# Regrouping the small products of a recurrence, a gated mixer and state updates between large products on one Trainium2 core

## The chip, the cores and the metric

The kernel runs on one core of a Trainium2 chip. The metric is the device time of one execution in microseconds, lower is better. Five engines work side by side, each with its own queue of instructions: TensorE (PE; its weight loads are listed apart as PEld), VectorE (DVE), ScalarE (ACT), GpSimd (POOL) and SyncE (SP), which only issues DMAs here. They wait for one another through semaphores.

## What is computed

One layer of a hybrid diffusion backbone, for 512 latent tokens and 128 context tokens (640 tokens, feature width 1024). Four token mixers run in parallel on projections of the same normalized input, and a convolutional feed-forward network follows. Cut to what the change touches:

```
proj = h @ w_in                                   # 13 sections: a_x a_b a_c b_q b_ff b_fb b_i b_g c_q c_k c_v d_u d_v
y_b  = hgrn2_bidir(b_q, b_ff, b_fb, b_i, b_g)     # gated linear recurrence, forward and backward
y_c  = attention(c_q, c_k, c_v)                   # neighbourhood attention
y_d  = d_u * (ws @ rmsnorm(d_v) + b)              # chunked gated MLP, per group of 64 columns
merged = g_a*(y_a@w_br_a) + g_b*(y_b@w_br_b) + g_c*(y_c@w_br_c) + g_d*(y_d@w_br_d)
```

The recurrence keeps for each of 4 heads a state of 64 x 64 and returns the final states of the context tokens too. In chunks of 128 tokens it is

```
scores(t, s) = sum_d q[t,d] * k[s,d] * prod of the gates f between s and t     (s <= t; mirrored backward)
state'       = (product of the gates) * state + k_decayed^T v
out          = scores @ v + (q * decay) @ state
```

## The kernel before

**Large products.** A section of w_in (256 columns) is two units, each 16 groups of three products (high and low parts of a float32 number, `gemm_half`, L370, moving 320 columns; `tok_tile`, L937, moving 256). They follow one another on TensorE in the order ff fb q i g dv du ck cq cv ac ax ab. After each three products stands `tick(us)` (L101).

**Small products between them.** The mixers are Python generators. `tick` adds the estimated time of the three products to a clock, `now`, and lets every generator whose time has come do its next step; `yield x` says how long it rests (times a factor: 1.3 for the recurrence, 1.4 for the gated MLP). The time at which a step is due counts from the clock before the last step, and a step's own products move the clock too, by `pe(us)`:

```
    def step(j):
            j[0] = now[0] + (next(j[1]) or 0.0) * j[2]
```

So a step's small products stand in the program between two groups of three large ones, at a place set by the clock, which is a plan and no measurement. Outside the boot part and the part that begins in `g_all` (L1427), where the order is pinned, the framework then settles the order of instructions on each engine before the run, by its own estimate of when inputs and buffers are ready; an instruction that comes earlier in the program goes first when both are ready. At run time each engine works in that order and waits where something isn't there.

**The recurrence** (`hgrn`, L460) builds the scores in seven levels, l = 0 to 6. From level 1 on, for each head parity `par` (rows 0 to 63 or 64 to 127) 40 products of 64 rows by 32 columns are made (L539), each of which the trace records twice, being float32. At level 6 the products are 64 rows by 64 columns and come in four groups of 10, two halves `s0` with two parities each. Each parity's group goes into a PSUM bank of its own (`pm()`), of which there are four. VectorE then merges it into the scores through a mask (L544), and makes the next level's keys and queries from the present ones (L555 to L562), which the next level's products read. Between the parities the generator rests 0.4 (3 at level 4), after a level 5 (`HD[1]`).

Then the states: for four pairs of chunks (forward, backward) `kt_load` transposes the keys on TensorE (2 transposes, L579) and ScalarE copies them into one of two slots; `upd` multiplies them with the values (2 products, L588) and VectorE adds into the running state (L599). Then the outputs, one 128-token tile after another in the order 4, 1, 2, 0, 3 (L629 to L646), with their root mean squares on VectorE and GpSimd; then five pairs of transposes (L659 to L668).

**The gated MLP** (`gmlp`, L681): five token tiles with four products each of 128 rows by 64 columns (L700), whose result VectorE takes (L705). It begins behind section du and runs at the same time as the recurrence.

**First gated pair** (`g_pair0`, L1264), pinned. `gprod` (L1208) makes twelve products (four quarters k of three) for one of seven combinations, `bprod` (L1218) three. Around the touched place: the third product into bank b3, then combination 6 into bank p1_, which ScalarE copies to y, then combination 5 into c2_, then combination 7 added into p1_. That last one can't begin before p1_ has been copied.

```
        gprod(b3, 0, 3, True)
        ...
        bprod(p1_, 0, 6, False)
        oact(y[:, 0:HC], p1_, AF.Copy)
        ...
        bprod(c2_, 0, 5, True)
        bprod(p1_, 0, 7, False)
```

Of the kernel before, what the change touches and what calls it, by code (L numbers as in the profile page):

```python
# [69 lines left out]
def tile_step(ctx: ExitStack, tc: tile.TileContext, a: dict, outs: list, dbg=None):  # L70
# [244 lines left out]
    def rstd(out, ss, n, inv):  # L315
        vec.tensor_scalar(out, ss, inv, EPS, ALU.mult, ALU.add)
        pool.tensor_tensor(out, out, neghalf[:, 0:n], ALU.pow)  # L317
# [142 lines left out]
    def hgrn():  # L460
# [51 lines left out]
        for l in range(7):  # L512
            B = 1 << l
            e_, x_ = blk(kk[:, 0], B), blk(kk[:, 1], B)
            r_, p_ = blk(qq[:, 0], B), blk(qq[:, 1], B)
            f_, g_ = blk(ff[:, 0], B), blk(ff[:, 1], B)
            nb = 1280 // (2 * B)
            if l == 0:
                m = yield from along(near)
                vec.copy_predicated(nat, lmask[:, 0, :].unsqueeze(1).to_broadcast([P, 20, 32]), bc(m))  # L520

            W = 64 if l == 6 else 32
            ns = 320 // W
            for s0, par in ([(s_, r) for s_ in range(0, 10, ns) for r in range(2)] if l else ()):
                b = slice(64 * par, 64 * par + 64)
                m = pm()
                for i in range(s0, s0 + ns):
                    for g in range(P // W):
                        d, t0 = (0, W * g) if l < 5 else (1 - g % 2, W * (g ^ 1))
                        t0 += (i % 5) * P  # L530
                        k0 = i * P + W * g
                        rhs = qq[b, d, i // 5, t0:t0 + W]
                        if l < 5:
                            lhs = kl[b, k0:k0 + W]
                            rhs = bass.AP(rhs.tensor, rhs.offset,
                                          [list(rhs.ap[0]), [2 * B, 16 // B], [1280 + B, 2], [1, B]])
                        else:
                            lhs = f2(kk[:, g % 2])[b, k0:k0 + W]
                        mm(m[W * g:W * g + W, (i - s0) * W:(i - s0 + 1) * W], lhs, rhs,  # L539
                           start=True, stop=True, tile_position=(64 * par, W * g))  # L540
                    pe(0.18)
                mv = m[:, 0:ns * W].rearrange("p (i t) -> p i t", t=W)
                if l < 5:
                    vec.copy_predicated(near_at[:, par], lmask[:, l, :].unsqueeze(1).to_broadcast([P, 10, 32]), mv)  # L544
                else:
                    for g in range(P // W):
                        c = slice(W * g, W * g + W)
                        act(at[c, par, s0:s0 + ns, W * (g ^ 1):W * (g ^ 1) + W], mv[c], AF.Copy)
                if par == 0:
                    yield 3 if l == 4 else 0.4  # L550
            if l == 4:
                for g in range(4):
                    c = slice(32 * g, 32 * g + 32)
                    act(at[c, :, :, c].rearrange("p r i t -> p (r i) t"), nat[c], AF.Copy)
            ups = ((e_[:, :, 0, :], f_[:, :, 1, 0:1]), (x_[:, :, 1, :], g_[:, :, 0, 0:1]),  # L555
                   (p_[:, :, 1, :], f_[:, :, 0, 0:1]), (r_[:, :, 0, :], g_[:, :, 1, 0:1]))
            for i, (dst, mul) in enumerate(ups):
                vec.tensor_tensor(dst, dst, mul.to_broadcast([P, nb, B]), ALU.mult)
                if i == 1 and l < 4:
                    kl = keys(l + 1)  # L560
            fa = ff.rearrange("p d n t -> p (d n t)").rearrange("p (n j i) -> p n j i", j=2, i=B)
            vec.tensor_tensor(fa[:, :, 0, 0], fa[:, :, 0, 0], fa[:, :, 1, 0], ALU.mult)  # L562
            yield HD[1]
# [36 lines left out]
                                                 tot[b, d, pr, t:t + 1], u, ALU.mult, ALU.add)  # L600

        assert "i_done" in R
        for f, bwd in ((0, 3), (1, 2), (2, 1), (4, 4)):
            kt_load(0, f, 0)
            kt_load(1, bwd, 1)
            yield 1.5
            upd(0, f, 0)
            upd(1, bwd, 1)
            yield 1
        for par in range(2):  # L610
            for d in range(2):
                nc.sync.dma_start(o_st[0, 0, d, par::2].rearrange("h k v -> k h v"),
# [12 lines left out]
                              ALU.mult)  # L625

        last = None
        for t in (4, 1, 2, 0, 3):
            m = pm()  # L629
            for pr in range(2):  # L630
                if t < 4:
                    o = m[:, pr * P:(pr + 1) * P]
                    mm(o, qq[:, 1, pr, t * P:(t + 1) * P], sreg[:, 0, t, pr, :], start=True, stop=False,
                       skip_group_check=True)
                    mm(o, qq[:, 0, pr, t * P:(t + 1) * P], sreg[:, 1, t, pr, :], start=False, stop=False,
                       skip_group_check=True)
                    pe(0.43)
                for par in range(2):
                    h = pr * 2 + par
                    mm(m[:, h * 64:(h + 1) * 64], at[:, par, pr * 5 + t, :],  # L640
                       vt[:, t * 256 + h * 64:t * 256 + (h + 1) * 64],
                       start=(t == 4), stop=(t == 4 or par == 1), skip_group_check=True)
                    pe(0.21)
            act(og[:, t * 256:(t + 1) * 256], m[:, 0:256], AF.Copy)
            act(o2[:, t * 256:(t + 1) * 256], m[:, 0:256], AF.Square)
            yield 0.5  # L646

            s4 = ss[:, 4 * t:4 * t + 4]
            vec.tensor_reduce(s4, o3(o2, t), AX.X, ALU.add)
            rstd(s4, s4, 4, 1.0 / 64)  # L650
            if last is not None:
                normed(last)
            last = t
        R["hgrn_out"] = True
        yield 2.5
        normed(last)
# [2 lines left out]
        for t in range(5):  # L659
            m = pm()  # L660
            for pr in range(2):
                ten.transpose(m[:, pr * P:(pr + 1) * P],
                                    og[:, t * 256 + pr * P:t * 256 + (pr + 1) * P], ident)
                pe(0.11)
                s = sg[:, pr * T + t * P:pr * T + (t + 1) * P]
                vec.scalar_tensor_tensor(s, m[:, pr * P:(pr + 1) * P],
                                         p1[:, C_HN + pr:C_HN + pr + 1], s, ALU.mult, ALU.mult)
            yield 0.4  # L668
        nc.sync.dma_start(ybd, split_y("D", sg).bitcast(F32))
        R["hgrn_done"] = True  # L670
        R["yd"] = split_y("E", R["yt"])
# [9 lines left out]
    def gmlp():  # L681
        du = R["DX0"][:, 0:1280]
        x1 = R["DX1"]
        vg, yt = x1[:, 0:1280], x1[:, 1280:2560]
        gg = region("G", [P, 1280])
        wst, brow = gg[:, 0:512], gg[:, 512:768]
        nc.sync.dma_start(wst, a["gmlp_ws"])
        for g in range(4):
            nc.sync.dma_start(brow[64 * (g % 2):64 * (g % 2) + 64, (g // 2) * P:(g // 2 + 1) * P],
                              a["gmlp_b"][0, g, :].partition_broadcast(64))  # L690
        ss = dss
        rstd(ss[:, 0:5], ss[:, 0:5], 5, 1.0 / 256)
        for t in range(5):
            v = vg[:, t * 256:(t + 1) * 256]
            vec.tensor_scalar(v, v, ss[:, t:t + 1], None, ALU.mult)
        yield 6
        for t in range(5):
            m = pm()
            for g in range(4):
                mm(m[64 * (g % 2):64 * (g % 2) + 64, (g // 2) * P:(g // 2 + 1) * P],  # L700
                   vg[:, t * 256 + 64 * g:t * 256 + 64 * g + 64], wst[:, g * P:(g + 1) * P],
                   start=True, stop=True)
                pe(0.21)
            for pr in range(2):
                vec.scalar_tensor_tensor(yt[:, pr * T + t * P:pr * T + (t + 1) * P],  # L705
                                         m[:, pr * P:(pr + 1) * P],
                                         p1[:, C_GN + pr:C_GN + pr + 1],
                                         brow[:, pr * P:(pr + 1) * P], ALU.mult, ALU.add)
            yield 0.4
        vec.tensor_tensor(yt, yt, du, ALU.mult)  # L710
        R["yt"] = yt
        pool.dma_start(ydd, yt)
# [492 lines left out]

    omm = Ordered(nc.tensor).matmul

    def gprod(o, p_, i, first):  # L1208
        u, n = GPROD[i]
        w = gw[p_, u]  # L1210
        xh_, xl_ = gx["x"][i]
        for k in range(4):
            for j, (h, x) in enumerate(((0, xh_), (0, xl_), (1, xh_))):
                omm(o, w[:, h, n, k, :], x[:, k, :], start=(first and k == 0 and j == 0),
                   stop=(k == 3 and j == 2), skip_group_check=True)
# [48 lines left out]
    def g_pair0(r):  # L1264
# [38 lines left out]
        g_sig(0, 0, ga[:, HC:T], ga[:, HC:T])  # L1303
        ovec.tensor_tensor(gb[:, HC:T], b2, gb[:, HC:T], ALU.subtract)
        r[2] = gp_load(2)
        gprod(b3, 0, 3, True)
        g_al(1, r[1])
        y = gw[0, "y"] = gp.tile([P, T], F32, tag="gt", name=nm("y"))
        c2_ = gw[0, "b2"] = pm()[:, 0:HC]
        bprod(p1_, 0, 6, False)  # L1310
        oact(y[:, 0:HC], p1_, AF.Copy)
        ovec.tensor_tensor(gb[:, 0:HC], b3, gb[:, 0:HC], ALU.add)
        bprod(c2_, 0, 5, True)
        bprod(p1_, 0, 7, False)
# [1345 lines left out]
```

## Time and profile before

| | before |
|---|---|
| median of 3 runs | 996.89 us (996.79 to 997.28) |
| the profiled execution | 997.16 us, its span 995.3 us |
| TensorE clock granted | 0.998 of full speed |
| recurrence's levels (L539) on TensorE | first product at 111.0 us, last at 158.2 us |
| gated MLP's products (L700) | 150.6 to 158.8 us |
| state updates (L579, L588) | 164.4 to 179.3 us |
| outputs (L633 to L640) | 180.3 to 190.0 us |
| transposes (L662) | 201.1 to 205.2 us |
| pair 0 (`g_pair0`) begins | 275.0 us |

How to read it: times in the trace count from the start of the span. In the timeline, a row has the start, the time covered, the engine, the line, the operation, what is written and read, the rows and columns of the array (64*32), the moving operand and the number of instructions. Lines of helpers that pin the order all appear as L150. Large products follow one another more closely than they last, since they are pipelined, so the distances of their starts are what counts.

### The profile page before, as it was taken

Reading aid. Unit: us, or ns where it says so; the run is one execution under the profiler, and the core shown is the slowest. Engines: PE = TensorE matmul, PEld = TensorE weight load, DVE = VectorE, ACT = ScalarE, POOL = GpSimd, SP = SyncE. Lnnn points to the kernel's source line nnn. Section 1 sums busy time; section 2 is a strip of 40 time slices with the busy share of each in tenths; the row PEclk is TensorE's granted clock in tenths of the full one; section 3 lists DMA queues with packets and bytes.
Section 4 is the critical chain, followed back from the end, with each engine's and each line's share of the span. In section 5 each row is a group of like instructions: output and inputs, shape, how many; then the busy total and the mean of one; then the engine's idle time right before and its main releaser. Section 6 shows DMA issues by size and latency. Waiting matters only on the chain.

```text
span 995.3 us, 19011 instructions
## 1 busy us (share of the span) xinstructions
PE 983.9 (99%) x7437; PEld 932.0 (94%) x7437; DVE 862.3 (87%) x1411; ACT 592.2 (59%) x1034; POOL 198.9 (20%) x272
## 2 busy tenths in 40 slices
PE   8999999999999999999999999999999999999997
PEld 6899999999999999999998899999999999888886
DVE  5779899879988789898877788999999998999796
ACT  6652343355575565555655476877777777756672
POOL 1000023414123122333300021322222222100004
PEclk9999999999999999999999999999999999999999
DMA  9886449898179789999958684766666666976842
GB/s 353 333 282 252 130 131 282 236 277 269 52 255 278 202 214 312 254 267 279 271 195 341 248 321 136 221 172 167 177 171 162 177 171 194 361 265 201 297 133 106
DMA packets 76857, 227.54 MB, mean 229 GB/s; under 512 B 10560, under 2 KB 25440, under 8 KB 74080
## 3 DMA queue, kind: packets, MB, share of 16 engines
q1 hardware_dynamic: 44832, 149.91, 42.8%
q0 software_dynamic: 31936, 76.43, 32.3%
q8 instruction: 58, 0.95, 0.4%
q14 instruction: 31, 0.25, 0.1%
HBM read 185.26 MB, written 61.36 MB: 248 GB/s over the span
## 4 chain that ended last, share of the span: by engine, by line
PE 93%; DVE 3%; DMA 2%; POOL 1%; issue 1%; ACT 0%; SPq 0%; POOLq 0%
PE m L150 22%; PE g L1728 21%; PE g L374 12%; PE m L2191 9%; PE m L1728 5%; PE g L150 5%; PE m L1480 4%; PE g L2191 4%; PE g L955 2%; PE g L1480 1%; PE m L539 1%; PE m L1723 1%; DMA A<-in_w_ada_dram 1%; PE m L882 1%; POOL hss L317 1%
## 5 line engine op out<-in xcount | busy, mean ns | idle before, releaser
L374 PE MATMUL g<-XH,w 128*128 128x320 f32 x576 | 140.5, 318 | 0.0
L374 PEld LDWEIGHTS g<-XH,w 128*128 128x128 f32 x576 | 98.8, 188 | 2.2 <-issue 1.0
L150 PE MATMUL m<-XH,w 128*128 128x320 f32 x416 | 98.7, 311 | 0.0
L374 PE MATMUL g<-XL,w 128*128 128x320 f32 x288 | 89.1, 310 | 0.0
L150 PEld LDWEIGHTS m<-XH,w 128*128 128x128 f32 x416 | 70.8, 188 | 1.7 <-ACT XH L150 0.6
L150 PE MATMUL m<-XL,w 128*128 128x320 f32 x208 | 63.0, 310 | 0.0
L2191 PE MATMUL m<-w,XH 128*128 128x512 f32 x246 | 58.5, 390 | 0.0
L2191 PEld LDWEIGHTS m<-w,XH 128*128 128x128 f32 x246 | 46.1, 188 | 9.6
L374 PEld LDWEIGHTS g<-XL,w 128*128 128x128 f32 x288 | 54.3, 188 | 0.3 <-issue 0.2
L150 DVE TENSOR_TENSOR w<-raw,w 128x640 fp32r<-128x640 f32 (+3 forms) x47 | 48.4, 1047 | 1.6 <-ACT w L150 1.5
L150 POOL DMA_DIRECT2D wsum<-in_w_dn_dram x36 | 37.6, 1275 | 59.2 <-issue 38.0
L150 ACT ACTIVATE w<-raw 128x640 fp32r<-128x640 f32 (+3 forms) x53 | 48.3, 931 | 1.8 <-DMA raw<-in_w_in_dram 1.5
L150 DVE SCALAR_TENSOR_TENSOR X<-X,p2t,X 128x641 f32<-128x641 f32 x44 | 38.8, 883 | 0.9
L150 DVE SCALAR_TENSOR_TENSOR X<-MG,p2t,X 128x641 f32<-128x641 f32 x44 | 38.9, 883 | 0.8
L150 PEld LDWEIGHTS m<-XL,w 128*128 128x128 f32 x208 | 38.6, 188 | 0.6 <-issue 0.6
L1728 PE MATMUL g<-XL,w 128*128 128x320 f32 x240 | 38.7, 310 | 0.0
L1728 PE MATMUL g<-XL,C 128*128 128x320 f32 x240 | 38.3, 309 | 0.0
L150 ACT ACTIVATE gb<-m 128x320 f32<-128x320 f32 x32 | 14.0, 437 | 40.7 <-PE m L150 40.6
L1728 PEld LDWEIGHTS g<-XL,w 128*128 128x128 f32 x240 | 35.9, 188 | 0.9 <-ACT MG L2088 0.4
L1728 PEld LDWEIGHTS g<-XL,C 128*128 128x128 f32 x240 | 36.0, 188 | 0.0
L150 ACT ACTIVATE X<-X,p2t 128x641 f32<-128x641 f32 x22 | 20.4, 927 | 18.7 <-DVE X L150 18.7
L150 ACT ACTIVATE X<-g 128x320 f32<-128x320 f32 x30 | 13.1, 436 | 30.3 <-PE g L1728 30.3
(622 smaller groups left out, 2948.5 us busy)
## 6 DMA issues: line engine op xcount, KB each, us to landing
wsum<-in_w_dn_dram POOLq DMA_DIRECT2D x30, 512.0 KB, 14.2
raw<-in_w_gp_dram SPq DMA_DIRECT2D x23, 640.0 KB, 7.7
raw<-in_w_up_dram SPq DMA_DIRECT2D x28, 512.0 KB, 5.3
raw<-in_w_in_dram SPq DMA_DIRECT2D x19, 512.0 KB, 5.5
H<-in_w_adt_dram SPq DMA_DIRECT2D x19, 512.0 KB, 4.7
G<-in_w_up_dram SPq DMA_DIRECT2D x12, 512.0 KB, 5.2
raw<-wsum SPq DMA_DIRECT2D x12, 512.0 KB, 5.9
actx<-X POOLq DMA_DIRECT2D x22, 256.0 KB, 4.9
```

Source lines behind the costliest of these rows:

```text
L150: r = f(*args, **kw)
L317: pool.tensor_tensor(out, out, neghalf[:, 0:n], ALU.pow)
L374: mm(o, w[:, h, k0 + k, :], r(k)[:, s], start=(k == 0 and i == 0), stop=(k == kt - 1 and i == 2))
L539: mm(m[W * g:W * g + W, (i - s0) * W:(i - s0 + 1) * W], lhs, rhs, start=True, stop=True, tile_position=(64 * par, W * g))
L882: mm(mo[64 * hh_:64 * hh_ + 64, 0:P], v, ptt[(u + hh_) % 4][:, j * P:(j + 1) * P], start=(j == 0), stop=(j == 2))
L955: mm(o, x(kx)[:, ts], w[:, h, k, :], start=(kx == 0 and i == 0), stop=(kx == 7 and i == 2))
L1480: mm(m, mh[MHN[q]][:, hx, k % 2, t * P:(t + 1) * P], wo[q][:, hw, k % 2, :], start=(k == 0 and i == 0), stop=(k == 7 and i == 2))
L1723: mm(o, w[:, k, :], x[:, k, :], start=(first and not part and k == 0 and j == 0), stop=(part == 1 and k == 3), skip_group_check=True)
L1728: z = mm(o, w[:, k, :], x[:, k, :], start=(first and k == 0 and j == 0), stop=(k == 3 and j == 2), skip_group_check=True)
L2191: mm(ps, s[t // 4][:, hx, k, o:o + P], w[:, hw, k, c0:c1], start=first, stop=i == 2 and bi == len(batch) - 1 and k == len(ks) - 1, skip_gr ...
```

## The change

The same instructions are issued, in other groups. In the levels, the rest between the parities stays only at level 4 and once at level 6. In the state updates, the update of one pair of chunks and the transposes of the next go into one step. The outputs go in groups of one, two and two token tiles, the last transposes and the gated MLP's tiles in groups of two, two and one with twice the rest. In `g_pair0`, the last quarter of the third product is issued behind combination 6.

```diff
-                if par == 0:
-                    yield 3 if l == 4 else 0.4
+                if (l, par) == (4, 0):
+                    yield 3
+                elif (l, par, s0) == (6, 1, 0):
+                    yield 0.4
...
-        for f, bwd in ((0, 3), (1, 2), (2, 1), (4, 4)):
-            kt_load(0, f, 0)
-            kt_load(1, bwd, 1)
-            yield 1.5
-            upd(0, f, 0)
-            upd(1, bwd, 1)
-            yield 1
+        ends = ((0, 3), (1, 2), (2, 1), (4, 4))
+        for i in range(5):
+            for d in range(2):
+                if i:
+                    upd(d, ends[i - 1][d], d)
+            for d in range(2):
+                if i < 4:
+                    kt_load(d, ends[i][d], d)
+            yield 1 + 1.5 * (i < 4)
...
-        for t in (4, 1, 2, 0, 3):
+
+        def outs(t):
             m = pm()
...
             act(o2[:, t * 256:(t + 1) * 256], m[:, 0:256], AF.Square)
-            yield 0.5
-
-            s4 = ss[:, 4 * t:4 * t + 4]
-            vec.tensor_reduce(s4, o3(o2, t), AX.X, ALU.add)
-            rstd(s4, s4, 4, 1.0 / 64)
-            if last is not None:
-                normed(last)
-            last = t
+
+        for ts_ in ((4,), (1, 2), (0, 3)):
+            for t in ts_:
+                outs(t)
+            yield 0.5 * len(ts_)
+            for t in ts_:
+                s4 = ss[:, 4 * t:4 * t + 4]
+                vec.tensor_reduce(s4, o3(o2, t), AX.X, ALU.add)
+                rstd(s4, s4, 4, 1.0 / 64)
+                if last is not None:
+                    normed(last)
+                last = t
...
-            yield 0.4
+            if t % 2 or t == 4:
+                yield 0.8
...
-    def gprod(o, p_, i, first):
+    def gprod(o, p_, i, first, ks=range(4)):
...
-        for k in range(4):
+        for k in ks:
...
-        gprod(b3, 0, 3, True)
+        gprod(b3, 0, 3, True, range(3))
         g_al(1, r[1])
...
         bprod(p1_, 0, 6, False)
         oact(y[:, 0:HC], p1_, AF.Copy)
+        gprod(b3, 0, 3, True, range(3, 4))
         ovec.tensor_tensor(gb[:, 0:HC], b3, gb[:, 0:HC], ALU.add)
```

The edit of the rest (`if t % 2 or t == 4`) stands twice, in the recurrence's transposes and in `gmlp`.

More of the change, by code (lines that the diff above doesn't have):

```diff
@@ L708, in gmlp @@
                                          brow[:, pr * P:(pr + 1) * P], ALU.mult, ALU.add)
-            yield 0.4
+            if t % 2 or t == 4:
+                yield 0.8
         vec.tensor_tensor(yt, yt, du, ALU.mult)
```

## The prediction

> **What bounds the kernel now.** I read the page first (busy shares), then the stretch from 120 to 160 us by the table of windows, then the timeline of TensorE visit by visit, and last the chain that ended last and the list of waits.
>
> ```profile
> span 995.3 us, 19011 instructions
> ## 1 busy us (share of the span) xinstructions
> PE 983.9 (99%) x7437; PEld 932.0 (94%) x7437; DVE 862.3 (87%) x1411; ACT 592.2 (59%) x1034; POOL 198.9 (20%) x272
> ```
> ```profile
> 120.00:160.00 40.00, 40.00 (x876) 36.31 (x864) 40.00 (x78) 18.65 (x37) 12.20 (x17) 1.00 0.56 175
> ```
>
> TensorE has work for 983.9 of 995.3 us, so time can only be won by making its stream denser. The second row is the stretch in which most of the touched products lie: PE 40.00 of 40 us, its weight loads 36.31, and VectorE (the third engine) also 40.00. TensorE sets the pace there, but VectorE has no reserve at all. That is the main danger.
>
> The profiled execution took 997.16 us: the span of 995.3 and 1.86 around it. It lies 0.27 over the median of 996.89. I work out differences in the span and take them from the median.
>
> **What a visit costs.** I call a run of small products between two large ones a visit. Its price: from the start of the last large product before it to the start of the second one after it, less two spacings of large products. The second one is needed because the slow start after a visit shows only there. First the recurrence's products (L539), which use 64 rows by 32 columns of the array; spacing of the 256-column products around them is 0.12 (119.17 to 119.29).
>
> ```profile
> 110.79 0.28 PE L955 MATMUL m<-w,XH 128*128 128x256 f32 x1
> 111.00 0.89 PE L539 MATMUL m<-C,D 64*32 64x32 f32 x80
> 111.82 0.38 PE L955 MATMUL m<-w,XH 128*128 128x256 f32 x1
> 112.04 0.28 PE L955 MATMUL m<-w,XL 128*128 128x256 f32 x1
> ```
> ```profile
> 119.17 0.28 PE L955 MATMUL g<-w,XL 128*128 128x256 f32 x1
> 119.29 0.28 PE L955 MATMUL g<-w,XH 128*128 128x256 f32 x1
> 119.50 0.64 PE L539 MATMUL m<-C,E 64*32 64x32 f32 x50
> 120.06 0.39 PE L955 MATMUL g<-w,XH 128*128 128x256 f32 x1
> 120.29 0.28 PE L955 MATMUL g<-w,XL 128*128 128x256 f32 x1
> ```
>
> 80 records cost 112.04 - 110.79 - 0.24 = 1.01 us, 50 cost 120.29 - 119.29 - 0.24 = 0.76. So a record costs 0.25 / 30 = 0.0083, and a visit 1.01 - 80 x 0.0083 = **0.34 us before its first product**. One sees it in the rows: 0.21 instead of 0.12 before the visit, 0.22 instead of 0.12 after the first large product. Now products on the whole array (transposes L579, state updates L588), with a spacing of 0.15 (154.70 to 154.85 in the fence on level 6 below):
>
> ```profile
> 164.21 0.31 PE L374 MATMUL g<-XH,w 128*128 128x320 f32 x1
> 164.35 0.60 PE L579 MATMUL m<-cst,B 128*128 128x128 f32 x4
> 164.71 0.39 PE L374 MATMUL g<-XH,w 128*128 128x320 f32 x1
> 164.94 0.30 PE L374 MATMUL g<-XL,w 128*128 128x320 f32 x1
> ```
> ```profile
> 166.39 0.31 PE L374 MATMUL g<-XH,w 128*128 128x320 f32 x1
> 166.54 1.05 PE L588 MATMUL m<-E,D 128*128 128x128 f32 x8
> 167.35 0.39 PE L374 MATMUL g<-XH,w 128*128 128x320 f32 x1
> 167.58 0.31 PE L374 MATMUL g<-XL,w 128*128 128x320 f32 x1
> ```
>
> 4 records cost 0.43, 8 cost 0.89: 0.115 each and 0.43 - 4 x 0.115 = -0.03, that is **nothing for the visit itself**. So only groups of products that use part of the array can gain by being put together.
>
> **The change part by part.**
>
> *Levels of the recurrence (L524 to L550).* At levels 1, 2, 3 and 5 the groups of both parities (80 records each) go into one visit; level 4 keeps two. Four visits fewer: 4 x 0.34 = **-1.36 us**. No instruction is added or dropped, and both parities read the same inputs, so no new wait arises at the second one. What the trace doesn't show is the step from rows 0 to 63 to rows 64 to 127 inside a 64x32 visit: between 0 and 0.34 (a whole visit's price, then the gain is nothing). I take 0, from the nearest row, the visit of level 6 below with 64x64: it holds both row halves (40 records, 1.24 us) and is no dearer per record than one half (20, 0.78). [...]
>
> *Level 6 and the gated mixer's products (L700).* Before, these share visits:
>
> ```profile
> 152.84 0.31 PE L374 MATMUL g<-XH,w 128*128 128x320 f32 x1
> 153.08 0.85 PE L539 MATMUL m<-C,B 64*64 64x64 f32 x20
> 153.86 0.66 PE L700 MATMUL m<-G,X 128*64 128x128 f32 x8
> 154.45 0.42 PE L374 MATMUL g<-XH,w 128*128 128x320 f32 x1
> 154.70 0.31 PE L374 MATMUL g<-XL,w 128*128 128x320 f32 x1
> 154.85 0.31 PE L374 MATMUL g<-XH,w 128*128 128x320 f32 x1
> 155.16 1.31 PE L539 MATMUL m<-C,B 64*64 64x64 f32 x40
> 156.40 0.66 PE L700 MATMUL m<-G,X 128*64 128x128 f32 x8
> ```
>
> 20 records take 0.78 to the next kind, 40 take 1.24: 0.023 each, and 0.32 left over at the change of kind (at least part of it a slow start, so 0.1 to 0.32). Before: five visits (the mixer's five token tiles), three of them with such a change. After: three mixer visits and two of level 6. If they fall apart, five visits and no change of kind: -0.3 to -0.96. If two coincide, two visits and one change fewer: -0.8 to -1.0. I take **-0.7**.
>
> *State updates (L603 to L609), outputs (L628 to L646), transposes (L659 to L668).* 8 visits become 5, 5 become 3, 5 become 3, all on the whole array: by the fence above **0**. What is late next: a visit of updates now asks for four of the four small PSUM banks, and two of them come free only when VectorE has done L599. Bounds -0.2 (the one wait of TensorE for VectorE in the transposes, quoted below, goes) to +0.4 (twice that wait at new places); I take 0.
>
> *Third product's last quarter (L1306).* Three products of 0.15 us move behind L1310, before L1313.
>
> ```profile
> 288.28 0.60 PE L150 MATMUL g<-MG,w 128*128 128x320 f32 x3
> ```
> ```profile
> 288.99 0.56 ACT L150 ACTIVATE ga<-ga,cst 128x320 f32<-128x320 f32 x1 [1.05 <-DVE ga L150]
> ```
> ```profile
> 289.45 0.42 ACT L150 ACTIVATE y<-g 128x320 f32<-128x320 f32 x1
> 289.93 0.71 PE L150 MATMUL g<-MG,S 128*128 128x320 f32 x3 [0.60 <-ACT y L150]
> ```
>
> TensorE waits at 289.93 for ScalarE's copy of y, because the next product writes the bank that is copied. The product that fills it (288.28) is over at 288.88 and would now be over 0.44 earlier. But y stands behind the sigmoid of ga in ScalarE's fixed order, and that waits for VectorE. The same 18 products lie ahead of the waiting one in either order, so it arrives no later and waits as long. **0**, bounds -0.44 (were the copy waiting for TensorE after all) and 0.
>
> Sum of the gains: 1.36 + 0.7 = 2.06 us.
>
> **What VectorE takes back.** The step list counts a step's own products toward its pause. A level's pause is 5 x 1.3 = 6.5; its last step now holds two groups of 1.8 instead of one, so 2.9 are left instead of 4.7. At 0.41 per three large products that is 8 threes instead of 12. The 12 stand in the chain that ended last as 36 products:
>
> ```profile
> 129.28 5.48 PE g L374 x36
> ```
>
> With the three between the parities gone, each of four level distances (1 to 2, 2 to 3, 3 to 4, 5 to 6) shrinks by 5 threes, 5 x 0.44 = 2.2 us, together 8.8. VectorE, full from 120 to 160, prepares each level's keys and queries and can't follow. The levels' products will be due up to some 9 us before their operands. What then? Instructions here that aren't pinned are ordered ahead of the run by an estimate of when their inputs are ready, and the trace shows that this works. The attention's sixth step, paced like the others, stood behind 40 large products where the one before had 21, in a stretch where VectorE was late too:
>
> ```profile
> 249.13 3.28 PE g L374 x21
> ```
> ```profile
> 254.72 6.06 PE g L374 x40
> ```
> ```profile
> PE m L662 <- DVE MG L666: 0.2, 1, 0.2
> ```
>
> So I expect large products to be put ahead, and only the error of that estimate to remain as a wait. The nearest measured wait of that kind is the third row, 0.2 us. Four levels become tight, and two further meetings (banks of the updates): between 0 and 6 x 0.2 = 1.2; I take three of six, **+0.6**.
>
> Forecast: -2.06 + 0.6 = -1.5 us, 996.89 - 1.5 = **995.4**. All that comes later moves along: the attention is started behind the last cv product (L929), not at the recurrence's end.
>
> **Rivals.**
> 1. *The gain comes whole.* VectorE's estimate fits, the 0.2 at L662 goes, the two mixer visits coincide: -2.06 - 0.2 - 0.3 = -2.6, 994.3. For it: in the old order the waits list has no L539 at all. Against: VectorE had just enough time then.
> 2. *VectorE becomes the bound (slower).* If the order keeps the levels at their due place, TensorE, which works in order, stands before L539 until VectorE has finished L558 of the level before, and with it every large product behind. Price up to the 8.8 us by which the levels move up; with the gain -2.06 that is +6.7, 1003.6 at the end and 999.2 if half is overtaken. It decides from 4.1 us of waiting on (2.06 + 2.0). Against it: the 40 products above.
> 3. *The change doesn't do what it says.* The ordering splits the groups again, as it already did with a level's 80 records (50 above). Then visits stay as many and the time stays: 996.9. For it: two parities need two free banks at once. Against: four banks, and the mixer and the recurrence share them already.
>
> **How the numbers follow.** Forecast (994.9 to 996.6) 0.47; rival 1, below 994.9, 0.28; rival 3 and small losses up to 998.9, 0.10; rival 2 beyond that 0.15. A measurement of this kernel tells about 0.2%, 2.0 us, from no change: faster means below 994.9, slower above 998.9. So faster 0.28, same 0.57, slower 0.15. The range 993.8 to 999.2 leaves out the best twentieth and most of rival 2.
>
> **What would show it.** Right: L539 in visits of 160 records at levels 1, 2, 3 and 5, each about 0.0083 x 160 + 0.34 = 1.67 us; L700 in groups of 16; L588 and L579 side by side with 0.115 a record as before; the wait at g<-MG,S still 0.6. Wrong: a visit of 160 dearer than 1.9 us (the row change has a price); TensorE in the waits list with L539 and VectorE, more than 1 us (rival 2 sets in); the wait for y gone (then it hung on TensorE). More than 2 us of difference after 300 us, where nothing was changed but the quarter, would mean that the ordering changed elsewhere, which I count at nothing.

## The result and the profile after

The changed kernel takes 1009.1 us (median, 1007.7 to 1010.6) against 996.8 (996.6 to 997.3): 1.0123 times as long, with an interval of 1.0105 to 1.014. The forecast was 995.4. The profiled execution has a span of 1007.3 us, 12.0 more than before. All times here and below are medians of undisturbed executions; one of levels_123_paced, the only one of that kernel with a trace, took 1948 us and is left out.

From the page of the changed kernel: the span, the busy times, and the granted clock in 40 slices of 25 us. Then the stretch that the prediction began with, from the table of windows.

```profile
span 1007.3 us, 19021 instructions
...
PE 987.8 (98%) x7437; PEld 934.8 (93%) x7437; DVE 862.9 (86%) x1411; ACT 593.7 (59%) x1034; POOL 197.9 (20%) x272
...
PEclk9999989999999999999999999999999999999999
```
```profile
120.00:160.00 40.00, 37.17 (x742) 35.34 (x742) 35.66 (x65) 19.84 (x41) 12.31 (x18) 0.91 0.57 165
```

The same 7437 products are there, and VectorE (DVE) works as long as before (862.9 for 862.3). But between 120 and 160 us both engines now stand still at times (37.17 and 35.66 of 40), and TensorE's clock is 0.91 instead of 1.00: they wait for one another in turn. Of the 876 records in this stretch only 742 are done. The list of TensorE's waits (in total, times, longest) names the places; of before it held, of the regrouped products, only 0.2 us at the transposes and the 0.6 us for y.

```profile
PE m L539 <- issue: 2.1, 1, 2.1
PE m L590 <- DVE D L601: 2.1, 1, 2.1
PE g L150 <- DVE F L150: 1.6, 1, 1.6
PE m L671 <- DVE MG L675: 1.5, 1, 1.5
PE m L876 <- DVE X L873: 1.3, 2, 1.1
...
PE m L539 <- DVE C L560: 0.6, 2, 0.4
```

The third row is of the start and was there before. The last one is the wait that the prediction counted on, of the levels' products for VectorE: 0.6 us in all. (Line numbers have moved: updates L588 are L590, transposes L579 are L581, VectorE's L599 is L601, the mixer's L700 is L710, the last transposes L662 are L671.)

**The visits themselves cost what the prediction said.** The timeline of level 1: 160 records in one visit.

```profile
110.16 0.28 PE L966 MATMUL m<-w,XH 128*128 128x256 f32 x1
110.37 1.58 PE L539 MATMUL m<-C,D 64*32 64x32 f32 x160
111.88 0.39 PE L966 MATMUL m<-w,XH 128*128 128x256 f32 x1
112.11 0.28 PE L966 MATMUL m<-w,XL 128*128 128x256 f32 x1
```

112.11 - 110.16 - 0.24 = 1.71 us against 1.67 forecast and 2.02 for the two of before (levels 1, 3 and 5 came as 160 records, level 2 as 14 and 146). The loss lies elsewhere. Level 3, and the clock behind it:

```profile
121.13 0.28 PE L966 MATMUL m<-w,XH 128*128 128x256 f32 x1
121.76 1.63 PE L539 MATMUL m<-C,D 64*32 64x32 f32 x132 [0.35 <-DVE C L560]
125.53 0.64 PE L539 MATMUL m<-C,D 64*32 64x32 f32 x28 [2.14 <-issue]
```
```profile
124.00:126.00 2.00, 0.47 (x28) 0.47 (x28) 0.69 (x3) 0.00 (x0) 0.00 (x0) 0.70 0.75 229
126.00:128.00 2.00, 2.00 (x20) 1.94 (x11) 1.78 (x4) 0.21 (x1) 0.00 (x0) 0.50 0.13 41
128.00:130.00 2.00, 2.00 (x10) 2.00 (x9) 2.00 (x4) 2.00 (x5) 0.00 (x0) 0.50 0.00 0
130.00:132.00 2.00, 2.00 (x10) 1.92 (x9) 2.00 (x4) 0.14 (x2) 0.00 (x0) 0.60 0.00 0
```

TensorE waits 0.35 us for VectorE, does 132 of the 160 records, stops for 2.14 us while the profile shows nothing that it waits for ("issue"), and its clock is at half (third number from the right: 0.50) for 6.8 us, from 124.8 us on, still inside the stop: 0.3 / 0.5 of the first row, two full rows, 0.4 / 0.5 of the last. A second low stretch, of 3.4 us, begins at 172.6. In the kernel before the clock stayed at 1.00 from 16 to 990 us. The third place, the state updates, on TensorE and on VectorE:

```profile
168.74 0.31 PE L374 MATMUL g<-XL,w 128*128 128x320 f32 x1
171.12 0.71 PE L590 MATMUL m<-E,D 128*128 128x128 f32 x4 [2.07 <-DVE D L601]
```
```profile
164.96 1.13 DVE L715 SCALAR_TENSOR_TENSOR X<-m,cst,G 128x128 f32<-128x128 f32 x4
168.70 1.23 DVE L284 SCALAR_TENSOR_TENSOR junk<-H,S 128x1024 bf16<-128x1024 f32 x1 [2.61 <-DMA H<-in_w_adt_dram]
169.85 0.08 DVE L284 DVE_READ_ACCUMULATOR junk<-H,S 128x1 f32 x1
169.85 2.46 DVE L601 SCALAR_TENSOR_TENSOR D<-D,tot,m 64x64 f32<-64x64 f32 x8
```

TensorE waits for L601, which frees a bank. L601 stands behind L284, a step of the modulation columns (`ada_cols`, L239), whose input H is still being loaded: VectorE does nothing for 2.61 us.

The mixer's groups, and the wait for y in pair 0, as the prediction named them:

```profile
161.31 0.31 PE L374 MATMUL g<-XH,w 128*128 128x320 f32 x1
161.54 1.09 PE L710 MATMUL m<-G,X 128*64 128x128 f32 x16
162.57 0.41 PE L374 MATMUL g<-XH,w 128*128 128x320 f32 x1
162.82 0.30 PE L374 MATMUL g<-XL,w 128*128 128x320 f32 x1
...
301.95 0.70 PE L150 MATMUL g<-MG,S 128*128 128x320 f32 x3 [0.69 <-ACT y L150]
```

A mixer visit of 16 costs 1.22 us where two of 8 cost 1.58, and the wait for y is 0.69 for 0.60.

**Where the time went.** The table adds up, from the timeline, the price of every visit as the prediction defined it, by kind, from the same large product at 99.1 us to the same one at 258.6 us (times of before); "large" is what the spacing of large products exceeds its normal value by, elsewhere. All in us; the kernels of the experiments are in it too.

| | median | levels 1-5 | level 6, mixer, updates | outputs | transposes | attention | large |
|---|---|---|---|---|---|---|---|
| before | 996.8 | 10.66 | 12.21 | 8.05 | 1.64 | 18.29 | 0.68 |
| after | 1009.1 | 12.66 | 16.58 | 8.04 | 3.03 | 19.80 | 3.13 |
| levels_only | 1006.9 | 12.51 | 14.71 | 8.05 | 3.21 | 19.35 | 2.24 |
| levels_paced | 997.9 | 10.08 | 12.05 | 8.05 | 1.63 | 19.69 | 0.69 |
| updates_only | 997.6 | 10.66 | 13.43 | 8.05 | 1.36 | 18.28 | 0.65 |
| mixer_only | 1001.6 | 10.66 | 15.20 | 8.45 | 1.85 | 18.27 | 0.65 |
| outputs_transposes_quarter | 998.1 | 10.66 | 12.24 | 8.05 | 2.80 | 18.62 | 0.69 |
| all_but_levels | 999.6 | 10.64 | 14.73 | 8.10 | 1.25 | 18.62 | 0.74 |
| shift_plus | 1008.6 | 9.40 | 16.57 | 8.05 | 3.22 | 19.86 | 2.19 |
| levels_123_near | 1003.9 | 9.69 | 13.50 | 8.05 | 1.89 | 23.96 | 1.24 |
| near_column_later | 997.3 | 9.69 | 13.32 | 8.05 | 1.75 | 18.29 | 0.66 |
| whole_change_paced | 996.8 | 10.06 | 12.14 | 8.05 | 1.26 | 19.61 | 0.74 |
| whole_paced_column | 996.4 | 10.07 | 12.14 | 8.05 | 1.27 | 18.33 | 0.72 |

A row of the table is one execution, the traced one, and the median is of all. After against before: 2.0 + 4.4 + 0 + 1.4 + 1.5 + 2.45 = 11.7 us. A large product lies 0.63 us earlier than before at 99 us, 11.10 later at 258.6 and 12.04 later at 297; from there to the end nothing is added.

### The profile page after: what moved, and what is told of

It reads as the page before. It is cut to its first block, busy times and chain, and to the rows that moved or that the text cites. A ratio compares the mean times of both kernels' runs of the same rounds, so it can differ in the third digit from the quotient of the medians.

```text
span 1007.3 us, 19021 instructions
## 1 busy us (share of the span) xinstructions
PE 987.8 (98%) x7437; PEld 934.8 (93%) x7437; DVE 862.9 (86%) x1411; ACT 593.7 (59%) x1034; POOL 197.9 (20%) x272
## 4 chain that ended last, share of the span: by engine, by line
PE 86%; DVE 6%; DMA 3%; issue 2%; POOL 1%; ACT 1%; SPq 0%; POOLq 0%; DVEq 0%
PE m L150 21%; PE g L1740 21%; PE m L2203 9%; PE g L374 9%; PE m L1740 5%; PE g L150 5%; PE m L1492 4%; PE g L2203 4%; PE g L966 2%; PE g L1492 1%; PE m L1735 1%; DMA A<-in_w_ada_dram 1%; DMA H<-in_w_adt_dram 1%; DVE junk L284 1%; DMA X<-in_w_adt_dram 1%
## 5 line engine op out<-in xcount | busy, mean ns | idle before, releaser
L2102 DVE TENSOR_TENSOR w<-raw,w 128x1024 fp32r<-128x1024 f32 (+1 forms) x26 | 29.1, 1118 | 2.6 <-ACT w L2098 2.6
```

Source lines behind the costliest of these rows:

```text
L2102: vec.tensor_tensor(w[:, 1, 0:n], raw, w[:, 0, 0:n].bitcast(F32), ALU.subtract)
```

## The experiments

**The parts alone.** First the levels as in the change, the levels with a longer rest behind them, the state updates as in the change, and the change without the levels.

The kernel before, with (levels_only)

```diff
-                if par == 0:
-                    yield 3 if l == 4 else 0.4
+                if (l, par) == (4, 0):
+                    yield 3
+                elif (l, par, s0) == (6, 1, 0):
+                    yield 0.4
```

and on top of it (levels_paced)

```diff
-            yield HD[1]
+            yield 7.0 if l in (1, 2, 3, 5) else HD[1]
```

The kernel before, with (updates_only)

```diff
-        for f, bwd in ((0, 3), (1, 2), (2, 1), (4, 4)):
+        ends = ((0, 3), (1, 2), (2, 1), (4, 4))
+        for i in range(5):
...
```

all_but_levels is the changed kernel with the first of these edits undone.

> Only the levels' groups of both parities are put together (levels 1, 2, 3, 5 in one visit each, level 6 in two); all else as before. Theory P (pacing and a stop of TensorE): the levels fall due too early; at level 3 TensorE stops some 2 us inside the visit and the granted clock is 0.5 for some 6 us after it. Of the 12.7 us that the large products lose in the changed kernel, about 6 lie there: 1002 to 1004 us, with a visit of 160 records that costs over 4 us and a stretch of 120 to 140 us with a granted clock under 0.95. Theory U (the state updates and what follows carry the loss, the stop is an accident of where the code lies): 995.5 to 997, all visits of 160 records at 1.7 us, clock 1.00.

> The same groups of levels, with the rest after levels 1, 2, 3 and 5 lengthened from 5 to 7, so that some 14 groups of three large products stand between two levels as before (3 + 12). Theory P: VectorE has its time again, the visits of 160 records cost 1.7 us each, and the gain of four merges comes, 995 to 996 us. Theory G (the long visit itself stops TensorE, whatever stands between): still 4 us and more over the kernel before, 1001 to 1004, with a stop inside a visit and a low clock behind it. Theory U: 995.5 to 997.

> Only the state updates are regrouped (update of one pair and transposes of the next in one step). Theory U and P alike: they ask for four banks at once and wait for VectorE once for about 2 us, and the clock falls for some microseconds behind it; 999 to 1001 us. If the wait came only because the levels had moved everything (the loss belongs to the levels alone), 996.5 to 997.5.

> The whole change without the levels' part (level groups as before). Theory P: the levels' 6 us are gone and the rest of the loss stays, 1001 to 1004 us. Theory U: nearly all of the loss stays, 1007 to 1010. If the levels carry it all by pushing everything behind them into VectorE's way: 996 to 998.

Measured: levels_only 1006.9 us (1.0100 times, 1.0085 to 1.0115), levels_paced 997.9 (1.0009, 0.9999 to 1.0018), updates_only 997.6 (1.0007, 0.9998 to 1.0017), all_but_levels 999.6 (1.0033, 1.0021 to 1.0046). The levels alone cost 10.1 us, more than the 6 expected, and without them 2.8 us of the 12.3 stay, less than the 4 to 7 of theory P. In levels_only the same stop stands at the same record (132), with a clock of 0.5 for 3.4 us behind it:

```profile
127.01 0.44 PE L539 MATMUL m<-C,D 64*32 64x32 f32 x28 [2.41 <-issue]
```

With the rest lengthened by 2 units, 9.0 of the 10.1 us go: so it is the pace and not the group. Theories U and G fall. The timeline of levels_paced at level 3:

```profile
127.36 1.58 PE L539 MATMUL m<-C,D 64*32 64x32 f32 x160
128.87 0.41 PE L374 MATMUL g<-XH,w 128*128 128x320 f32 x1
```

There is no stop. The gain did not come though: at level 5 TensorE waits 0.49 us for VectorE's L560, and the attention costs 1.4 us more (table). In updates_only the wait that was taken for 2 us is 0.8 (timeline of TensorE):

```profile
170.94 1.05 PE L588 MATMUL m<-E,D 128*128 128x128 f32 x8
172.05 0.44 PE L579 MATMUL m<-cst,B 128*128 128x128 f32 x2
173.30 0.44 PE L579 MATMUL m<-cst,B 128*128 128x128 f32 x2 [0.81 <-DVE D L599]
```

It is the fourth bank: after the updates (two banks) and the first transposes (one) TensorE stands until VectorE has freed another. The other visits of 12 records cost 1.33, which is 0.44 + 0.89, what their two parts cost apart.

**Is the stop a wait for instructions?** The page has 58 transfers of the kind "instruction" on queue 8, 0.95 MB, 16.4 KB each, and TensorE has 14,874 records of products and weight loads, 256.4 for each transfer. From this count I estimate that TensorE's instructions come in blocks of 256. In the changed kernel, between 122 and 125 us, the table of queues shows

```profile
q8 instruction: 1, 0.02, 2.1%
```

one such transfer of 0.021 x 16 x 3 = 1.0 us; in the trace's list it begins at 123.12, where 132 records end at 123.39 and the rest begin at 125.53. A visit of 160 records has 320 instructions (each record is a product with its weight load): it is longer than such a block. So two kernels with only the count of idle bf16 products at the very start altered, which moves all later instructions against the blocks:

```diff
-WARM = 100
+WARM = 124
```

in shift_plus, and 92 in shift_minus, both on top of levels_only.

> The levels' part alone (as in levels_only), with 124 instead of 100 of the idle products at the very start: 48 TensorE instructions more, which lie in a wait of the start and move every later instruction by 48 places. Theory F (the stop is a wait for instructions: TensorE's instructions come in blocks of 256; at level 3 it stood before L539 for VectorE just at a block edge, so the next block was ordered late, and the visit of 320 instructions, two to a record, runs through the 256 that were there in 1.5 us): the edge now lies 40 places before the visit, the block is ordered in time, the stop of 2.41 us is gone, and with it the low clock. 1002 to 1004 us against 1006.9. Theory V (the stop is VectorE's doing, a wait that the records don't name, or something of the levels as such): the stop of 2.4 us stays at 132 products, 1006 to 1008.

> The levels' part alone, with 92 instead of 100 idle products at the start: every later instruction 16 places earlier. Theory F: the block edge lies 24 instead of 8 places inside the visit of level 3, the block is still ordered late, and the visit stops after 140 products instead of 132, for about 2.3 us; 1006 to 1008 us. Theory V: it stops after 132 as before.

Measured: shift_minus 1009.6 us (one run), shift_plus 1008.6 (1.0128, 1.0097 to 1.0159). The timeline of level 3 in shift_minus, then in shift_plus:

```profile
122.43 1.55 PE L539 MATMUL m<-C,D 64*32 64x32 f32 x140 [0.37 <-DVE C L560]
126.66 0.53 PE L539 MATMUL m<-C,D 64*32 64x32 f32 x20 [2.69 <-issue]
```
```profile
128.89 1.59 PE L539 MATMUL m<-C,D 64*32 64x32 f32 x160
130.41 0.39 PE L957 MATMUL m<-w,XH 128*128 128x256 f32 x1
```

Sixteen instructions fewer ahead of it, and the stop comes after 140 records instead of 132: 8 records and their 8 weight loads later, as theory F had it. It is a stop at a place in the code and no wait for data.

In shift_plus level 3 has no stop, but the stop is not gone. It ends 2.7 us ahead of level 3, between large products, as the list of waits and the timeline of TensorE show:

```profile
PE g L957 <- issue: 1.3, 1, 1.3
```
```profile
124.44 0.40 PE L957 MATMUL g<-w,XH 128*128 128x256 f32 x2
126.15 0.28 PE L957 MATMUL g<-w,XL 128*128 128x256 f32 x1 [1.30 <-issue]
```

Counted from the kernel's first product, the one behind the stop is number 1492 in the changed kernel, in levels_only and in shift_minus, and number 1364 in shift_plus: 128 products, which with their loads are 256 instructions, or one block of the estimate, apart. Edges are counted from there in steps of 128 products. The traces also show when such a stop came. In all four the transfer of the block began 0.85 to 1.10 us after TensorE had passed the edge before it, took 1.0 to 1.4, and the first product ran 1.4 to 1.6 after it had landed, while the block ahead had been run in 1.1 to 2.1 us (in the changed kernel: edge at 122.08, transfer at 123.12, 1.04 later, in 1.00 us, first product 1.41 after it had landed, the block ahead run in 1.31). In the kernel before the transfer began 0.86 us after the same edge (123.08), the block ahead took 5.48 us, and there was no stop. At level 1 of the changed kernel a block was run in 1.4 us too, but the next one's transfer had begun 1.9 us ahead of the edge, and there was no stop. That TensorE waits at these places for the next block is my estimate from these times. Theory V, as put on record (a stop of VectorE's doing, at 132 products), falls: in shift_plus no product of levels 1 to 3 waits for VectorE.

The expected gain missed: 1008.6 us, not 1002 to 1004. This says little of the stop, because 4.8 us were lost before the levels began: TensorE waited 1.07 us for ScalarE at 80 us and then ran at half clock until 92.5. From 99 to 258.6 us shift_plus loses 7.75 us against the kernel before, levels_only 8.55. The clock did not fall behind this stop (1.00 from 94 us on), and the levels cost 9.40 us, 1.26 less than before (the stop, between large products, is in "large"). But a wait for VectorE comes at level 6 (timeline of shift_plus):

```profile
148.59 0.31 PE L374 MATMUL g<-XH,w 128*128 128x320 f32 x1
150.00 0.30 PE L539 MATMUL m<-C,B 64*64 64x64 f32 x2 [1.11 <-DVE C L560]
```

Level 6, mixer and updates cost 1.9 us more than in levels_only. This fits a stop that is a part of the loss and not its root: TensorE, let through at one place, meets VectorE at a later one.

**The other parts alone.** The mixer's groups; the outputs, last transposes and the quarter together.

```diff
-            yield 0.4
+            if t % 2 or t == 4:
+                yield 0.8
```

in `gmlp` (mixer_only), and

```diff
+        for ts_ in ((4,), (1, 2), (0, 3)):
...
-        gprod(b3, 0, 3, True)
+        gprod(b3, 0, 3, True, range(3))
...
```

with the transposes' rest as in the change (outputs_transposes_quarter), both on the kernel before.

> Only the gated mixer's token tiles in groups of two, two and one. The whole change without the levels was 2.8 us slower, the state updates alone 0.8; in the former a visit of level 6 and 16 mixer records cost 3.70 us with waits for VectorE and ScalarE inside, and mixer and level 6 together 8.26 instead of 6.78. Theory M (the mixer's groups ask for two more banks in the stretch where level 6 needs its own, and TensorE waits): 998 to 999 us. If the waits came from the moved state updates: 996.3 to 997.2.

> Only the outputs in groups, the last transposes in groups and the third product's last quarter. My steps gave all three nothing; in the trace of the kernel without the levels' part the outputs cost 8.10 us (8.05 before), the transposes 1.25 (1.64) and the wait for y 0.6 as before. So 996.2 to 997.0; 998 or more would say that one of them costs in a way that the other parts hid.

Measured: mixer_only 1001.6 us (1.0050, 1.0033 to 1.0066), outputs_transposes_quarter 998.1 (1.0014, 1.0005 to 1.0024). Both are dearer than expected. The mixer's second pair in the timeline of mixer_only:

```profile
152.70 0.79 PE L539 MATMUL m<-C,B 64*64 64x64 f32 x18 [0.35 <-DVE C L558]
153.42 0.66 PE L700 MATMUL m<-G,X 128*64 128x128 f32 x8
154.72 0.66 PE L700 MATMUL m<-G,X 128*64 128x128 f32 x8 [0.64 <-DVE X L705]
```

The first two mixer tiles, level 6 and a third tile hold the four banks, and the next tile waits until VectorE has taken the first (L705). That is theory M. Behind it VectorE also stands 2.81 us at L284 for its load, as in the changed kernel, and the updates pay 1.5 us. The traced execution took 1000.3 us, with a clock of 0.999; the three others took 1001.5 to 1001.9 with 0.994, and what they lost more is in no trace. In outputs_transposes_quarter the outputs cost nothing more (8.05), the wait for y is 0.6 as before, and the transposes wait 1.43 us for L671 on VectorE, with no fall of the clock.

**How far it adds up, and a gain that goes missing.** The whole change with the longer rest; and only levels 1 to 3 merged, twice, with a rest of 7.5 and of 6.7.

The changed kernel with the longer rest of levels_paced is whole_change_paced. The kernel before with

```diff
-                if par == 0:
+                if par == 0 and l not in (1, 2, 3):
...
-            yield HD[1]
+            yield 6.7 if l in (1, 2, 3) else HD[1]
```

is levels_123_near, and with 7.5 levels_123_paced.

> The whole change, with the rest after levels 1, 2, 3 and 5 at 7 instead of 5. Parts measured alone, against 996.8: levels +10.1, levels with the longer rest +1.0, all the others +2.8. If the levels' pace carries the loss and the parts add up: 1000 to 1001.5 us, no stop at level 3 and a clock of 0.998. If the loss comes from groups as such: 1005 and more.

> Only the merges of levels 1, 2 and 3, with the rest after each of them lengthened so that the later visits stay where they were in the kernel before; levels 5 and 6 as before. My step, a visit's price of 0.34 us, three times: 995.9 us, if everything behind keeps its order. In levels_paced the four merges saved 0.58 us on the levels in the trace (a wait of 0.5 for VectorE at level 5 took the rest), and the attention behind lost 1.4. Should the attention's order change here too, 997 to 998.

> As levels_123_paced (1004.4 us, where its only trace is of a disturbed run and can't be read), with a rest of 6.7 instead of 7.5: every visit from level 3 on then stands within 4 places of where it stands in the kernel before, the mixer's and level 6's too. Theory D (a long rest put the levels too late, and the work behind them collided with the sections): three visits fewer at 0.34 us, 995.9 us, and 160 records at 1.7 us. Theory F (a merged visit that meets a block edge stops TensorE wherever it stands): 1000 to 1004, with a stop inside a visit of 160 and a clock of 0.5 behind it.

Measured: whole_change_paced 996.8 us (1.0002, 0.9993 to 1.0011): one line takes away all of the 12.3 us, where 8 to 9 had been expected. The parts do not add up (10.1 + 0.8 + 4.8 + 1.4 alone, 12.3 together, 2.8 without the levels, 0.1 paced). levels_123_paced 1003.5 (1.0069, 1.0052 to 1.0086), levels_123_near 1003.9 (1.0074, 1.0059 to 1.0089): the 995.9 of both missed by 8 us, so a longer rest alone is not enough. In the second the three merges bring exactly their price (9.69 for 10.66, 3 x 0.32), there is no stop in a visit as theory F would have it, and 85 us later, in the timelines of TensorE and of VectorE,

```profile
229.98 0.31 PE L374 MATMUL g<-XL,w 128*128 128x320 f32 x1
234.08 0.87 PE L865 MATMUL m<-cst,X 128*128 128x128 f32 x3 [3.79 <-DVE X L862]
```
```profile
226.66 1.00 DVE L854 TENSOR_REDUCE ast<-MG 128x1 f32<-128x384 f32 x2
231.10 1.23 DVE L284 SCALAR_TENSOR_TENSOR junk<-H,S 128x1024 bf16<-128x1024 f32 x1 [3.43 <-DMA H<-in_w_adt_dram]
```

the attention waits 3.79 us, again behind L284, and the clock is at half from 232.2 to 239.0 us (6.8 us, not the 3.4 of the expectation below). In the kernel before this step (column 38) ran at 218.7 us, ahead of the attention's tiles. Is it the cause? The kernel has a table of extra rests for columns; one more entry puts the step behind the next tile.

```diff
-COLWAIT = {39: 8}
+COLWAIT = {38: 8, 39: 8}
```

on top of levels_123_near (near_column_later) and of whole_change_paced (whole_paced_column).

> levels_123_near (1003.9 us) with one more edit: the column step 38 of L284 rests 8 longer, as step 39 already does. In levels_123_near the levels' stretch was 0.97 us shorter, as three visits of 0.33, but at 231 us TensorE waited 3.8 us for VectorE's L862, and VectorE stood there 3.43 us at L284 waiting for the load of H; a clock of 0.5 for 3.4 us followed. Theory C (a step of VectorE in fixed order, placed before its load has landed, holds up the attention): with L284 placed behind the next tile's L854 the wait is gone, 995.3 to 996.5 us. Theory R (the attention is late because the recurrence before it uses VectorE at other times, the load is only the last name): it waits for something else, 1000 or more.

> whole_change_paced (996.8 us) with the same edit of step 38. There TensorE waited 0.6 us for L873 in the attention and the attention's visits cost 1.3 us more than in the kernel before. Theory C: 995.3 to 996.3 us, under the kernel before. Theory R: 996.5 to 997.5, or another wait in its place.

Measured: near_column_later 997.3 us (1.0006, 0.9997 to 1.0015), whole_paced_column 996.4 (0.9995, 0.9986 to 1.0004). The attention is back at 18.29 and 18.33, what it cost before. The timeline of VectorE in near_column_later:

```profile
228.35 0.73 DVE L862 TENSOR_SCALAR MG<-MG,ast 128x384 f32<-128x384 f32 x2
230.85 1.02 DVE L852 TENSOR_TENSOR X<-m,B 128x384 f32<-128x384 f32 x2 [1.77 <-PE m L848]
...
235.18 1.22 DVE L284 SCALAR_TENSOR_TENSOR junk<-H,S 128x1024 bf16<-128x1024 f32 x1
```

L862 is done before L284, which no longer waits for its load. Theory C is shown, though both kernels end just above its range: 6.6 us hung on the place of one step. What is left is small: in near_column_later level 6 and the mixer take 1.2 back (waits of 0.6 for L558 and 0.4 for L705), and in pair 0 the wait for y is 1.1 instead of 0.6. whole_paced_column is the best version, and its 0.4 us cannot be told from no change.

## Why the prediction was wrong

- *Visit price, four merges, -1.36.* Right. A visit of 160 costs 1.70 to 1.72 (forecast 1.67); three merges brought 0.97, four 1.26 in shift_plus. The step from one row half to the other costs 0.05 at most, so the end of the bounds at which it cost a visit is out.
- *Level 6 and mixer, -0.7.* The size was right where VectorE was in time: 6.20 for 6.78 in whole_paced_column, without the updates. The step forgot that a pair of mixer tiles holds two of four banks until VectorE's L705: alone the groups of two cost 4.8 us. I had named the banks, in rival 3 only, and dismissed them there.
- *State updates, 0, bound +0.4.* The cause named (four banks, L599) was right, the bound too small: a wait of 0.81 and its restart, +1.22 in the trace. In the changed kernel the five visits became eleven, because large products were put between their halves, and one of them waited 2.07 us.
- *Outputs 0, quarter 0.* Right: 8.05 but for mixer_only's 8.45, and the wait for y stayed (0.69 in the changed kernel), as argued from ScalarE's order.
- *Transposes, 0, perhaps -0.2.* The 0.2 went in some kernels (1.25 for 1.64), and in others a wait of 1.4 for VectorE came: mis-sized in the bad direction.
- *What VectorE takes back, +0.6.* **This step failed.** It said that the framework's ordering would put large products ahead of levels that are due too early, from one case of the attention (40 products for 21), and that only waits of 0.2 us would remain, at the levels and the banks. The ordering did not: 28, 24 and 24 large products stand before levels 3, 4 and 6, where the prediction's own count of eight threes gives 24 and the kernel before had 39, 36 and 30. Level 3 began at 121.76 us, before at 126.94, and the shortened rest alone cost 9 us. The arithmetic before it (each of four distances shrinks by 2.2 us, VectorE can't follow) was right, and it was rival 2, to which I gave 0.15. The waits at the levels themselves came to 0.6 us, as large as forecast, so the sign by which the prediction wanted to know rival 2, more than 1 us of L539 waiting for VectorE, did not show. The loss stood at places that the step put at 0.2 or at nothing: the stop of 2.14, L601's bank 2.07, the transposes 1.47, the attention 1.3, and half clock for 10.2 us (6.8 and 3.4).
- *Rival 2's price, at most +6.7.* Too low, because it counted a wait at its length only. To it came a stop at a place in the code (2.14), half clock behind waits (2.45 under "large" alone), and L284 in VectorE's fixed order, which met its load at a bad time as soon as the steps before it moved. None of the three occurs between 99 and 300 us in the trace of before, so no row of that stretch could give its price; a wait of L284 for its load does stand in that trace earlier, 2.98 us before the step at 63 us, and the prediction had no term for it.
- *After 300 us nothing changes.* Right: 12.04 at 297 us, and the same to the end.

That L284's wait is the cause was tried at one place only (231 us); at 168 us in the changed kernel it is read from the trace. Why the transfer of a block begins 0.85 to 1.10 us behind some edges stays open: in three kernels a wait for VectorE of 0.35 to 0.37 us stood just ahead of the edge, in shift_plus none did. With four merges only one longer rest (7.0) was tried, and it moves every later step besides giving VectorE time, so how much of the 12.3 us each of the two brought back isn't separated.

## What to carry to other kernels

When small work is put together, the rest that its supplier gets must be set again: compute the new distance between steps and compare it with the busy share of the engine that prepares them; where that is full, lengthen the pause first (here: 1009.1 us without, 996.8 with). Where an order is settled before the run, a gain of 1 us in one place moves every later step (in levels_123_near 0.97 us in the levels, and a wait of 3.79 us some 85 us later), so look for steps in a fixed order that read a fresh load, because each is a possible stop for all that stands behind it. A wait of TensorE costs more than its length if the clock falls behind it (0.5 for 6.8 us at a stop of 2.14 in the changed kernel, but 1.00 behind a wait of 1.43 in outputs_transposes_quarter), so waits are to be priced from a trace in which they occurred.

## What the runs showed of the hardware

- The page of the changed kernel has 58 instruction transfers of 16.4 KB on queue 8 for 14,874 instructions of TensorE, 256.4 for each; the blocks of 256 are my estimate from that. Counted so, TensorE stopped at a block's edge for 2.14 (the changed kernel), 2.41 (levels_only) and 2.69 us (shift_minus) inside a visit of 160 records and for 1.30 between large products (shift_plus), each time where the transfer had begun 0.85 to 1.10 us after the edge before. The nine other visits of 146 to 160 records in the first three kernels had no stop, but for one of 0.26.
- The granted clock fell to 0.5 for 6.8 us at a stop of 2.14, and behind other stops and waits for 3.4 to 10.2 us; it fell behind a wait of 1.07 us in one kernel (shift_plus) and stayed at 1.00 behind one of 1.43 in another (outputs_transposes_quarter). At the seven falls between 16 and 990 us the stop or wait was 1.07 to 3.79 us long.
